# An expert layer in two chunks of 1792 features whose gate and up products share four PSUM banks, in place of four chunks with banks of their own

## The chip, the core and the metric

The kernel runs on one core of one Trainium2 chip. The metric is device time in microseconds (us) of one launch, the median of several runs. A change of under 0.2% (about 3 us here) can't be told from no change.

## The reference, cut to what matters

The reference is a trunk of two decoder layers over 256 tokens of width 1024. Each layer has a mixer (differential attention beside a gated DeltaNet) and a channel mixer: a dense SwiGLU in the first layer, and in the second a choice of two out of eight SwiGLU experts of 3584 features for each token. The change touches the experts alone.

```python
def swiglu(x, w_gate, w_up, w_down):
    return (jax.nn.silu(x @ w_gate) * (x @ w_up)) @ w_down

def moe_ffn(x, router_w, w_gate, w_up, w_down):
    ...
    logits = jnp.einsum('td,de->te', xf, router_w).astype(jnp.float32)
    top_val, top_idx = lax.top_k(logits, TOP_K)
    gates = jax.nn.softmax(top_val, axis=-1)
    ...
    def expert_block(args):
        tok_b, e_b = args
        xb = xf[tok_b]
        return swiglu(xb, w_gate[e_b], w_up[e_b], w_down[e_b])
    ...
    y = y * w_buf[:, None].astype(y.dtype)
    out = jax.ops.segment_sum(y, tok_buf, num_segments=T)
```

All weights are float32, and the eight experts hold 352 MB of them, each read once.

## The kernel before

**Numbers in two halves.** Products keep float32 accuracy by splitting both sides into a high and a low part of type float32r. A weight tile `raw` is loaded by a DMA on SyncE's queue (`load`), ScalarE copies it to the high part `wh` (L171), and VectorE subtracts to get the low part `wl` (L174). `halves` does this for one half of a load (2048 columns) at a time, so a half has 1024 columns, one ScalarE and one VectorE instruction, and `wpool` has four buffers for each part (`WB = 4`). For 128 tokens a half takes six matmuls of 512 columns: tokens high and low with `wh`, tokens high with `wl`.

**Jobs.** Each expert is a job. Five jobs are wide (128 slots for tokens). Three, the experts with the fewest tokens, are narrow: 64 slots, and high and low tokens lie side by side in one stationary tile of 128, so that a half takes four matmuls and not six. The sums of the two sides are joined later: ScalarE copies partitions 64 to 127 of a bank to SBUF (`lead`, L1099), and TensorE adds them to partitions 0 to 63 by a product with a shift matrix. The order of the jobs is wide, narrow, wide, narrow, wide, narrow, wide, wide (`TURN`).

**Chunks.** A job walks its 3584 features in chunks of 1024, 1024, 1024 and 512. For a chunk, all gate products run first into the banks `ps_mm`, then all up products into `ps_gd`. ScalarE takes SiLU of the gate banks into `hh` (L1144, L1148), VectorE multiplies `hh` with the up banks (L1155), TensorE transposes `hh` (L1168) into `ps_a`, and ScalarE and VectorE split the result into `hT` (L1170, L1171). The down products of a chunk (`down`, banks `ps_b`) are run one chunk later, mixed with the next chunk's transposes, so that TensorE has work while `hh` is made. In a narrow job the gate's leads run in the middle of the up products, when they are two or three pieces from their end.

**Dispatch and combine.** The tokens of a job are gathered by products with a 0/1 matrix `D` (`dispatch`, L99 `ps_a<-D,xs`, ScalarE copies to `xg`, L1016). It is called for a narrow and the following wide job at once, in eight steps that follow each other without other work between them, after the third chunk of the job before. `combine` scatters a finished job's sum back into `x_tok`.

**What sets the order.** The code is written in the order above. A scheduler may interleave instructions that don't depend on each other; an instruction marked with `pin` keeps its place on its engine. Each engine works its own list in order, so an instruction that waits holds up all behind it. Loads go through 13 buffers of 8 KB for each partition (`RING` and `RING2`).

Of the kernel before, what the change touches and what calls it, by code (L numbers as in the profile page):

```python
# [16 lines left out]
P = 128  # L17
# [20 lines left out]
RING2 = 6  # L38
SLOTS = "rrrrrxxxrrxxx"
CHUNKS = (1024, 1024, 1024, 512)  # L40
# [25 lines left out]
def trunk(ctx, tc, x, positions, w_in, conv_w, a_log, dt_bias, gdn_norm_w, lam_q1, lam_k1, lam_q2, lam_k2,  # L66
# [742 lines left out]
    def gate_pieces():  # L809

        n = 2048 // CHUNKS[0]
        wg = moe_w_gate[0, 0].rearrange("(k p) c -> p k c", p=P)
        return [piece(wg[:, k:k + n, 0:CHUNKS[0]], n, CHUNKS[0]) for k in (0, n)]

# [49 lines left out]
    def route(pl, mp):  # L864
# [8 lines left out]
        tie = mp.tile([P, NE, NE], F32, tag="hT0", name="tie")  # L873
# [101 lines left out]
    def experts(xs, jobs, mp, ring2, rest, first):  # L975
# [3 lines left out]

        C2 = [(sum(CHUNKS[:i]), n) for i, n in enumerate(CHUNKS)]  # L980

# [15 lines left out]
        def dispatch(group, early=False):  # L997
# [3 lines left out]
            Dt = mp.tile([P, NB, W], F32R, tag="hh", name=nm("D"))  # L1001
# [3 lines left out]
            for k in range(KD):  # L1005
# [11 lines left out]
            return xgs  # L1017

        def transposed(n):
            Dt = mp.tile([P, NB, P], F32R, tag="hh", name=nm("D"))  # L1020
# [8 lines left out]
        def in_pieces(w, c0, cols, parts=1, k0=0):  # L1029

            nk = 2048 // cols
            for k in range(k0, KD, nk):
                for j, wh, wl in piece(w[:, k:k + nk, c0:c0 + cols], nk, cols, parts):
                    yield k + j, nk // 2, wh, wl

        def products(outs, xg, narrow, k, nk, wh, wl, cols):

            if not narrow:
                xstat(outs, [xg[:, 0:4], xg[:, 4:8]], k, nk, 0, wh, wl, cols, KD)
                return  # L1040
            for j in range(nk):
                x_ = xg[:, k + j].rearrange("p c s -> p (c s)")
                for w in (wh, wl):
                    for i, o in enumerate(outs):
                        mm(o, x_, w[:, j * cols + i * 512:j * cols + (i + 1) * 512], k + j == 0 and w is wh, False)

        def down_pieces(e, c, parts=1, cut=1):
            wd = weights(e, 2).rearrange("(f p) d -> p f d", p=P)
            c0, cols = C2[c]
            for f in range(0, cols // P, 2):  # L1050
                last = f == cols // P - 2
                yield [(f + j, wh, wl) for j, wh, wl in piece(wd[:, c0 // P + f:c0 // P + f + 2, :], 2, D, parts,
                                                              cut if last else 1)]

        def down(subs, n, c, hT, py):
            f0 = C2[c][0] // P
            for f, wh, wl in subs:
                if jobs[n][3]:
                    x_ = hT[:, f].rearrange("p c s -> p (c s)")
                    for w in (wh, wl):  # L1060
                        for i, o in enumerate(py):
                            mm(o, x_, w[:, i * 512:(i + 1) * 512], f0 + f == 0 and w is wh,
                               f0 + f == FE // P - 1 and w is wl)
                else:
                    for w in (wh, wl):
                        for c_ in range(2 if w is wh else 1):
                            for i, o in enumerate(py):
                                mm(o, hT[:, f, c_], w[:, i * 512:(i + 1) * 512], f0 + f == 0 and w is wh and c_ == 0,
                                   f0 + f == FE // P - 1 and w is wl)

        def combine(n, q, py, DT):
            for i in range(2):
                ys = mp.tile([P, 2, 512], F32R, tag=f"hT{q % 2}", name=nm("ys"))
# [21 lines left out]
        def lead(p, room, i):  # L1095
# [8 lines left out]
        q = 0  # L1104
        xgs = dict(zip(groups[0], dispatch([jobs[n] for n in groups[0]], True)))
        groups.pop(0)
# [302 lines left out]
```

## Time and profile before

| what | value |
|---|---|
| median of 3 runs | 1533.79 us (1531.84 to 1534.95) |
| the profiled execution's own time | 1530.45 us |
| its span, first to last instruction | 1528.3 us |
| mean granted TensorE clock | 0.979 of full speed |

The span is the time between the first and the last instruction that the profiler saw; about 2 us lie around it. Engines are PE (TensorE; PEld is its weight load), DVE (VectorE), ACT (ScalarE) and SP (SyncE, which issues the loads). The expert layer takes the span from about 533 us to 1508 us.

### The profile page before, as it was taken

The page shows a single profiled execution, that of the slowest core. Times are in us where ns is not written, and L with a number is a line of the kernel's source. Part 1 is how long each engine was busy: PE and PEld are TensorE (multiplying, and loading weights), DVE is VectorE, ACT ScalarE, POOL GpSimd, SP SyncE. Part 2 cuts the span into 40 slices and gives each one's busy share as a digit, 9 for nine tenths or more (in the row PEclk, how much of TensorE's full clock was granted, in tenths as well). Part 3 has the DMA queues.
Part 4 walks back from the last instruction along what each step waited for, and adds up shares of the span by engine and source line. Part 5 has one row for each costly group of instructions (what it writes and reads, how often), then busy time and mean ns, then how long its engine had stood idle before and what let it go on. Part 6 is the DMA issues. An engine that isn't in the chain of part 4 may idle for free.

```text
span 1528.3 us, 23267 instructions
## 1 busy us (share of the span) xinstructions
PE 1459.9 (96%) x8522; PEld 1164.7 (76%) x8522; DVE 1248.0 (82%) x1553; ACT 1079.5 (71%) x1494; POOL 23.7 (2%) x36
## 2 busy tenths in 40 slices
PE   7989999999999999999999999999999999999996
PEld 7968899998978888765577775677776567877774
DVE  5787754556797889799999799999879999888996
ACT  3747544456657477788887788887778987777773
POOL 1000000000000000000000000000000000000000
PEclk8999999999999899999999999999999999999998
DMA  9623465545533589799999999999989999998960
GB/s 310 213 90 111 148 212 192 188 124 188 192 112 139 221 296 399 293 372 364 407 389 347 350 354 357 402 409 345 347 322 350 403 408 350 381 331 325 346 239 32
DMA packets 135522, 433.89 MB, mean 284 GB/s; under 512 B 7368, under 2 KB 9544, under 8 KB 135392
## 3 DMA queue, kind: packets, MB, share of 16 engines
q1 hardware_dynamic: 134208, 428.54, 75.7%
q0 software_dynamic: 1184, 3.71, 0.9%
q8 instruction: 71, 1.16, 0.3%
q14 instruction: 59, 0.48, 0.1%
HBM read 431.17 MB, written 1.05 MB: 283 GB/s over the span
## 4 chain that ended last, share of the span: by engine, by line
PE 82%; DVE 9%; ACT 4%; issue 2%; DMA 2%; SPq 0%; DVEq 0%; ACTq 0%
PE ps_gd L99 25%; PE ps_mm L99 25%; PE ps_b L99 21%; PE ps_a L99 9%; DVE wl L174 5%; ACT wh L171 2%; DMA raw<-in_moe_w_up_dram 1%; PE ps_a L1168 1%; DMA x_in<-in_x_dram 1%; DVE hT L1171 1%; DVE hh L1155 1%; DVE x_in L1082 1%; ACT xg L1016 0%; PE ps_mm L560 0%; DVE ys L1076 0%
## 5 line engine op out<-in xcount | busy, mean ns | idle before, releaser
L174 DVE TENSOR_TENSOR wl<-raw,wh 128x1024 fp32r<-128x1024 f32 (+1 forms) x811 | 956.7, 1218 | 154.0 <-ACT wh L171 148.9
L171 ACT ACTIVATE wh<-raw 128x1024 fp32r<-128x1024 f32 (+1 forms) x811 | 830.6, 1055 | 242.2 <-PE ps_gd L99 94.8
L99 PE MATMUL ps_b<-wh,hT 128*128 128x512 f32 x816 | 235.1, 400 | 0.3
L99 PE MATMUL ps_mm<-wh,xg 128*128 128x512 f32 x728 | 216.3, 404 | 2.4 <-ACT wh L171 2.4
L99 PE MATMUL ps_gd<-wh,xg 128*128 128x512 f32 x728 | 207.3, 394 | 0.0
L99 PEld LDWEIGHTS ps_b<-wh,hT 128*128 128x128 f32 x816 | 151.6, 189 | 38.1 <-ACT wh L171 3.1
L99 PE MATMUL ps_b<-wl,hT 128*128 128x512 f32 x492 | 164.3, 414 | 10.0 <-DVE wl L174 9.7
L99 PEld LDWEIGHTS ps_mm<-wh,xg 128*128 128x128 f32 x728 | 138.8, 193 | 35.1 <-ACT wh L171 4.1
L99 PEld LDWEIGHTS ps_gd<-wh,xg 128*128 128x128 f32 x728 | 136.7, 188 | 31.7
L99 PE MATMUL ps_mm<-wl,xg 128*128 128x512 f32 x448 | 150.1, 412 | 9.6 <-DVE wl L174 9.5
L99 PE MATMUL ps_gd<-wl,xg 128*128 128x512 f32 x448 | 148.3, 408 | 0.8 <-DVE wl L174 0.7
L99 PEld LDWEIGHTS ps_b<-wl,hT 128*128 128x128 f32 x492 | 86.7, 190 | 47.8 <-DVE wl L174 32.5
L99 PEld LDWEIGHTS ps_mm<-wl,xg 128*128 128x128 f32 x448 | 82.6, 192 | 47.4 <-DVE wl L174 31.2
L99 PEld LDWEIGHTS ps_gd<-wl,xg 128*128 128x128 f32 x448 | 80.3, 188 | 38.0 <-DVE wl L174 18.2
L99 PE MATMUL ps_mm<-xT,wh 128*128 128x256 f32 x448 | 70.9, 280 | 0.0
L1170 ACT ACTIVATE hT<-ps_a 128x512 fp32r<-128x512 f32 (+1 forms) x47 | 27.3, 583 | 53.5 <-PE ps_a L1168 53.3
L99 PEld LDWEIGHTS ps_mm<-xT,wh 128*128 128x128 f32 x448 | 60.8, 189 | 0.4
L1155 DVE TENSOR_TENSOR hh<-hh,ps_gd 128x512 f32<-128x512 f32 (+1 forms) x56 | 36.2, 681 | 26.3 <-PE ps_gd L99 21.8
L99 PE MATMUL ps_gd<-xT,wh 128*128 128x256 f32 x320 | 50.5, 280 | 0.0
L99 PE MATMUL ps_mm<-xT,wl 128*128 128x256 f32 x224 | 44.7, 280 | 0.0
L99 PEld LDWEIGHTS ps_gd<-xT,wh 128*128 128x128 f32 x320 | 43.1, 189 | 0.0
L1171 DVE TENSOR_TENSOR hT<-ps_a,hT 128x512 fp32r<-128x512 f32 (+1 forms) x47 | 31.2, 667 | 14.3 <-ACT hT L1170 14.3
(400 smaller groups left out, 1562.7 us busy)
## 6 DMA issues: line engine op xcount, KB each, us to landing
raw<-in_moe_w_gate_dram SPq DMA_DIRECT2D x110, 1024.0 KB, 6.5
raw<-in_moe_w_up_dram SPq DMA_DIRECT2D x110, 1024.0 KB, 7.6
raw<-in_moe_w_down_dram SPq DMA_DIRECT2D x110, 1024.0 KB, 8.2
raw<-in_w_in_dram SPq DMA_DIRECT2D x24, 1024.0 KB, 6.0
raw<-in_ffn_w_gate_dram SPq DMA_DIRECT2D x11, 1024.0 KB, 5.1
raw<-in_ffn_w_up_dram SPq DMA_DIRECT2D x11, 1024.0 KB, 5.2
raw<-in_ffn_w_down_dram SPq DMA_DIRECT2D x11, 1024.0 KB, 4.9
raw<-in_w_out_dram SPq DMA_DIRECT2D x8, 1024.0 KB, 4.8
```

What stands on the lines that cost most here:

```text
L99: return PE.matmul(o, lhsT, rhs, start=start, stop=stop, skip_group_check=True)
L171: high = S.activation(wh[:, c:c + n], w, AF.Copy)
L174: low = V.tensor_tensor(wl[:, c:c + n], w, wh[:, c:c + n].bitcast(F32), op=ALU.subtract)
L1082: V.scalar_tensor_tensor(o, pt, jobs[n][2][:, b], o, op0=ALU.mult, op1=ALU.add)
L1155: pin(V.tensor_tensor(h, h, p[rows, :], op=ALU.mult))
L1168: PE.transpose(pt[:, f * w:(f + 1) * w], hh[rows, (f0 + f) * P:(f0 + f + 1) * P], ident[rows, rows])
L1170: S.activation(hT[:, f0:f0 + n_, 0], pv, AF.Copy)
L1171: V.tensor_tensor(hT[:, f0:f0 + n_, 1], pv, hT[:, f0:f0 + n_, 0].bitcast(F32), op=ALU.subtract)
```

## The change

The features of a job are walked in two chunks of 1792. A gate or up load is one row block of 128 by 1792 (7 KB in one run for each partition), cut into two halves of 896, and a matmul has 448 columns. Gate and up use the same four banks (`ps_mm` twice and `ps_gd` twice), one after the other: the up products of a chunk can begin when SiLU has read the gate's banks. Three pieces of the former chunk's down products stand between gate and up, four after up. The leads of a narrow job move from the middle of the up products to the end of the gate and the end of the up (`leads`, two buffers `room`). A down load takes two neighbouring rows for each partition (8 KB in one run), which needs features in another order: the transposes read every 14th column of `hh`. The eight steps of a dispatch are put one by one behind the pieces of the job's last up products, and the transposes behind the pieces of the next gate products (`side`). `hT` is no longer double, and the load buffers are 12 instead of 13.

```diff
-RING2 = 6
-SLOTS = "rrrrrxxxrrxxx"
-CHUNKS = (1024, 1024, 1024, 512)
+RING2 = 5
+SLOTS = "rrrrrxxxrrxx"
+CHUNK = 1792
+BANK = CHUNK // 4
...
+        def in_pieces(w, c, k0=0):
+
+            for k in range(k0, KD):
+                yield k, piece(w[:, k:k + 1, c * CHUNK:(c + 1) * CHUNK], 1, CHUNK)
...
+            wd = weights(n, 2)[c * CHUNK:(c + 1) * CHUNK].rearrange("(p j) d -> p j d", j=NF)
...
+        def leads(banks):
 
             hi = slice(64, P)
-            o = room[hi, i * 512:(i + 1) * 512]
-            pin(S.activation(o, p[hi, :], AF.Copy))
-            return lambda: mm(p[0:64, :], shift[hi, 0:64], o, False, True)
+            moves = []
+            for p in banks:
+                o = mp.tile([P, BANK], F32R, tag="room", name=nm("room"), bufs=2)
+                pin(S.activation(o[hi], p[hi, :], AF.Copy))
+                moves.append(lambda o=o, p=p: mm(p[0:64, :], shift[hi, 0:64], o[hi], False, True))
+            return moves
...
+            hv = hh[rows].rearrange("s (p j) -> s j p", j=NF)
...
+                    PE.transpose(pt[:, f * w:(f + 1) * w], hv[:, f0 + f], ident[rows, rows])
...
+        def gu_banks():
+            return [bank(t)[:, 0:BANK] for t in ("mm", "mm", "gd", "gd")]
...
+                moves = leads(banks) if narrow else ()
+                more()
+                for move in moves:
+                    move()
+                for i, p in enumerate(banks):
+                    pin(S.activation(hh[rows, i * BANK:(i + 1) * BANK], p[rows, :], AF.Silu))
+                more()
+                more()
+                banks = gu_banks()
+                if c == NC - 1 and groups and n + 1 not in xgs:
+                    group = groups.pop(0)
+                    tiles, side = dispatch([jobs[g] for g in group])
+                    xgs.update(zip(group, tiles))
+                for sub in in_pieces(wu, c):
+                    products(banks, xg, narrow, *sub)
+                    if side:
+                        side.pop(0)()
...
+                moves = leads(banks) if narrow else ()
+                more()
+                for move in moves:
+                    move()
+                for i, p in enumerate(banks):
+                    h = hh[rows, i * BANK:(i + 1) * BANK]
+                    pin(V.tensor_tensor(h, h, p[rows, :], op=ALU.mult))
                 for subs in downs:
                     down(subs, *pend)
```

Place one is ScalarE's list in the first narrow job, its second chunk; `wh` rows are conversions, copies to `hT` (before) or `room` (changed) are leads, rows to `hh` are SiLU. Before, this is the stretch around the end of the up products:

```order
L1099 ACTIVATE hT_1005_7066<-ps_mm_1000_7061 64x512
L1099 ACTIVATE hT_1005_7066<-ps_mm_1001_7062 64x512
L171 ACTIVATE wh_1042_7197<-raw_1041_7195 128x1024
L171 ACTIVATE wh_1044_7207<-raw_1041_7195 128x1024
L171 ACTIVATE wh_1047_7217<-raw_1046_7215 128x1024
L171 ACTIVATE wh_1049_7221<-raw_1046_7215 128x1024
L1144 ACTIVATE hh_1004_7065<-ps_mm_1000_7061 64x512
L1144 ACTIVATE hh_1004_7065<-ps_mm_1001_7062 64x512
L1099 ACTIVATE hT_1005_7066<-ps_gd_1002_7063 64x512
L1099 ACTIVATE hT_1005_7066<-ps_gd_1003_7064 64x512
L171 ACTIVATE wh_1052_7243<-raw_1051_7241 128x1024
L171 ACTIVATE wh_1054_7247<-raw_1051_7241 128x1024
```

In the changed kernel this is the stretch around the end of the gate products (`raw_1124` and later are down pieces):

```order
L173 ACTIVATE wh_1125_7495<-raw_1124_7493 128x1024
L1101 ACTIVATE room_1120_7485<-ps_mm_1073_7316 64x448
L1101 ACTIVATE room_1121_7487<-ps_mm_1074_7317 64x448
L173 ACTIVATE wh_1127_7499<-raw_1124_7493 128x1024
L1101 ACTIVATE room_1122_7489<-ps_gd_1075_7318 64x448
L1101 ACTIVATE room_1123_7491<-ps_gd_1076_7319 64x448
L1165 ACTIVATE hh_1119_7484<-ps_mm_1073_7316 64x448
L1165 ACTIVATE hh_1119_7484<-ps_mm_1074_7317 64x448
L1165 ACTIVATE hh_1119_7484<-ps_gd_1075_7318 64x448
L1165 ACTIVATE hh_1119_7484<-ps_gd_1076_7319 64x448
L173 ACTIVATE wh_1130_7521<-raw_1129_7519 128x1024
L173 ACTIVATE wh_1132_7525<-raw_1129_7519 128x1024
```

The gate's two leads stood four conversions ahead of the SiLU that needs them. Now all four leads and all four SiLU stand together, with a single conversion among them, and the third lead can begin only when the first has been read by TensorE, since there are two `room` buffers.

Place two is VectorE's list in the same chunk, around the product of `hh` with the up banks. Before:

```order
L174 TENSOR_TENSOR wl_1048_7218<-raw_1046_7215,wh_1047_7217 128x1024
L174 TENSOR_TENSOR wl_1050_7222<-raw_1046_7215,wh_1049_7221 128x1024
L1155 TENSOR_TENSOR hh_1004_7065<-hh_1004_7065,ps_gd_1002_7063 64x512
L1155 TENSOR_TENSOR hh_1004_7065<-hh_1004_7065,ps_gd_1003_7064 64x512
L174 TENSOR_TENSOR wl_1053_7244<-raw_1051_7241,wh_1052_7243 128x1024
```

Changed (`wl_1182` is the last up half; `wl_1189` and `wl_1191` are down halves, whose `wh` stands behind two leads on ScalarE's list):

```order
L176 TENSOR_TENSOR wl_1182_7696<-raw_1178_7685,wh_1181_7695 128x896
L176 TENSOR_TENSOR wl_1189_7714<-raw_1187_7711,wh_1188_7713 128x1024
L176 TENSOR_TENSOR wl_1191_7718<-raw_1187_7711,wh_1190_7717 128x1024
L1185 TENSOR_TENSOR hh_1119_7484<-hh_1119_7484,ps_mm_1139_7555 64x448
L1185 TENSOR_TENSOR hh_1119_7484<-hh_1119_7484,ps_mm_1140_7556 64x448
L1185 TENSOR_TENSOR hh_1119_7484<-hh_1119_7484,ps_gd_1141_7557 64x448
L1185 TENSOR_TENSOR hh_1119_7484<-hh_1119_7484,ps_gd_1142_7558 64x448
L176 TENSOR_TENSOR wl_1194_7740<-raw_1192_7737,wh_1193_7739 128x1024
```

The product stands behind two down halves in both, and has four instructions and not two.

Place three is TensorE's list in a dispatch for a narrow and a wide job. Before, all 32 matmuls stand in one row; the first eight of them:

```order
L99 MATMUL ps_a_882_6565<-D_879_6560,xs0_5508 128x192
L99 MATMUL ps_a_882_6565<-D_879_6560,xs1_5509 128x192
L99 MATMUL ps_a_882_6565<-D_879_6560,xs0_5508 128x192
L99 MATMUL ps_a_882_6565<-D_879_6560,xs1_5509 128x192
L99 MATMUL ps_a_883_6572<-D_879_6560,xs0_5508 128x192
L99 MATMUL ps_a_883_6572<-D_879_6560,xs1_5509 128x192
L99 MATMUL ps_a_883_6572<-D_879_6560,xs0_5508 128x192
L99 MATMUL ps_a_883_6572<-D_879_6560,xs1_5509 128x192
```

Changed, in the next such dispatch, the first of its steps between two up pieces:

```order
L101 MATMUL ps_gd_1412_8628<-wh_1420_8647,xg_855_6439 128x448
L101 MATMUL ps_gd_1413_8629<-wh_1420_8647,xg_855_6439 128x448
L101 MATMUL ps_gd_1412_8628<-wl_1421_8648,xg_855_6439 128x448
L101 MATMUL ps_gd_1413_8629<-wl_1421_8648,xg_855_6439 128x448
L101 MATMUL ps_a_1422_8657<-D_1414_8630,xs0_5508 128x192
L101 MATMUL ps_a_1422_8657<-D_1414_8630,xs1_5509 128x192
L101 MATMUL ps_a_1422_8657<-D_1414_8630,xs0_5508 128x192
L101 MATMUL ps_a_1422_8657<-D_1414_8630,xs1_5509 128x192
L101 MATMUL ps_mm_1410_8626<-wh_1424_8666,xg_855_6439 128x448
L101 MATMUL ps_mm_1411_8627<-wh_1424_8666,xg_855_6439 128x448
L101 MATMUL ps_mm_1410_8626<-wh_1424_8666,xg_855_6439 128x448
L101 MATMUL ps_mm_1411_8627<-wh_1424_8666,xg_855_6439 128x448
```

Four matmuls of the dispatch now follow twelve of the up products, eight times.

## Rows read from the trace of the kernel before

**Rows 1.** The page, part 1: busy time, share of the span and instructions of each engine.

```profile
PE 1459.9 (96%) x8522; PEld 1164.7 (76%) x8522; DVE 1248.0 (82%) x1553; ACT 1079.5 (71%) x1494; POOL 23.7 (2%) x36
```

**Rows 2.** Busy time of each engine (count) in nine stretches, from one SiLU to the next.

```profile
core 0: us, PE busy (x) PEld busy (x) DVE busy (x) ACT busy (x) POOL busy (x), PEclk, DMA share, GB/s
612.88:644.04 31.16, 29.37 (x138) 24.00 (x137) 22.00 (x22) 21.99 (x37) 0.00 (x0) 0.95 0.74 271
819.53:854.00 34.47, 34.47 (x156) 28.00 (x155) 31.30 (x30) 26.53 (x30) 0.00 (x0) 1.00 1.00 377
854.00:883.86 29.86, 28.00 (x138) 22.44 (x137) 22.00 (x22) 21.88 (x37) 0.00 (x0) 1.00 0.83 304
912.84:943.01 30.17, 27.32 (x109) 17.62 (x108) 28.29 (x30) 24.99 (x29) 0.00 (x0) 1.00 0.92 344
943.01:974.00 30.99, 29.91 (x112) 18.64 (x111) 29.79 (x30) 28.02 (x31) 0.00 (x0) 0.94 1.03 401
974.00:996.83 22.83, 21.74 (x81) 13.88 (x80) 21.14 (x21) 19.01 (x22) 0.00 (x0) 0.93 1.03 409
996.83:1027.95 31.12, 30.46 (x127) 22.50 (x126) 29.47 (x27) 25.93 (x27) 0.00 (x0) 1.00 1.03 409
1094.17:1125.63 31.46, 29.61 (x138) 23.85 (x136) 22.00 (x22) 21.98 (x37) 0.00 (x0) 0.95 0.78 289
1335.55:1363.80 28.25, 27.73 (x137) 22.29 (x136) 21.79 (x21) 20.55 (x30) 0.00 (x0) 1.00 0.87 321
```

**Rows 3.** Chain that ended last, in order of time, one wide chunk: start, us, what.

```profile
833.97 11.12 PE ps_mm L99 x48
```

**Rows 4.** TensorE in order of time, dense stage, 256-column matmuls: start, us.

```profile
301.06 0.64 PE L99 MATMUL ps_gd<-xT,wh 128*128 128x256 f32 x4
301.54 0.40 PE L99 MATMUL ps_gd<-xT,wl 128*128 128x256 f32 x2
301.78 0.64 PE L99 MATMUL ps_gd<-xT,wh 128*128 128x256 f32 x4
```

**Rows 5.** Groups by line and form, 540 to 1500 us, VectorE.

```profile
L174 DVE TENSOR_TENSOR wl<-raw,wh 128x1024 fp32r<-128x1024 f32 x662 | 776.0, 1217 | 49.0 <-ACT wh L171 47.9
...
L1155 DVE TENSOR_TENSOR hh<-hh,ps_gd 64x512 f32<-64x512 f32 x21 | 13.5, 676 | 14.5 <-PE ps_gd L99 14.5
```

**Rows 6.** The same for ScalarE.

```profile
L171 ACT ACTIVATE wh<-raw 128x1024 fp32r<-128x1024 f32 x663 | 676.4, 1056 | 112.8 <-PE ps_mm L99 45.1 <-PE ps_gd L99 33.4 <-DVE wl L174 15.0
...
L1099 ACT ACTIVATE hT<-ps_gd 64x512 fp32r<-64x512 f32 x21 | 11.5, 590 | 1.6 <-PE ps_gd L99 1.1
```

**Rows 7.** Groups by line, whole span.

```profile
L1168 PEld LDWEIGHTS ps_a<-cst,hh 128*128 128x128 f32 (+1 forms) x224 | 24.0, 140 | 10.1 <-DVE hh L1155 4.2 <-issue 1.1
...
L799 DVE TENSOR_TENSOR hT<-sg,hT 128x256 fp32r<-128x256 f32 x20 | 8.4, 420 | 0.8 <-ACT hT L798 0.6
```

**Rows 8.** All engines in order of time, end of a narrow job's second up phase.

```profile
935.50 10.31 DVE L174 TENSOR_TENSOR wl<-raw,wh 128x1024 fp32r<-128x1024 f32 x9
...
943.88 0.62 PE L99 MATMUL ps_gd<-wl,xg 128*128 128x512 f32 x2
...
944.37 1.08 ACT L1099 ACTIVATE hT<-ps_gd 64x512 fp32r<-64x512 f32 x2 [0.29 <-PE ps_gd L99]
...
945.48 2.01 ACT L171 ACTIVATE wh<-raw 128x1024 fp32r<-128x1024 f32 x2
...
946.53 0.67 PE L99 MATMUL ps_gd<-hT,shift 64*64 64x512 f32 x2
947.01 1.28 DVE L1155 TENSOR_TENSOR hh<-hh,ps_gd 64x512 f32<-64x512 f32 x2 [1.20 <-PE ps_gd L99]
```

**Rows 9.** All engines in order of time, inside a dispatch.

```profile
871.08 0.52 PEld L99 LDWEIGHTS ps_a<-D,xs 128*128 128x128 f32 x4 [0.87 <-ACT xg L1016]
...
872.47 0.97 PEld L99 LDWEIGHTS ps_a<-D,xs 128*128 128x128 f32 x8 [0.87 <-ACT xg L1016]
```

**Rows 10.** Who waited for whom, 560 to 1500 us: total, times, longest.

```profile
ACT wh L171 <- DMA raw<-in_moe_w_up_dram: 0.6, 2, 0.3
```

More of the change, by code (lines that the diff above doesn't have):

```diff
@@ L1004, in dispatch, with part @@
             xgs = [xg_tile(job[3]) for job in group]
-            for k in range(KD):
+            def part(k):
                 pt = bank("ab"[k % 2] if early else "a")
@@ new lines, in products @@
+        def products(outs, xg, narrow, k, parts):
+            for i, (_, wh, wl) in enumerate(parts):
+                o = outs[2 * i:2 * i + 2]
+                if not narrow:
+                    xstat(o, [xg[:, 0:4], xg[:, 4:8]], k, 1, 0, wh, wl, CHUNK // 2, KD)
+                    continue
+                x_ = xg[:, k].rearrange("p c s -> p (c s)")
+                for w in (wh, wl):
+                    for j in range(2):
+                        mm(o[j], x_, w[:, j * BANK:(j + 1) * BANK], k == 0 and w is wh, False)
@@ L1055, in down, with down_pieces @@
+        def down_pieces(n, c, first=0, parts=1, cut=1):
+            wd = weights(n, 2)[c * CHUNK:(c + 1) * CHUNK].rearrange("(p j) d -> p j d", j=NF)
+            for f in range(first, NF, 2):
+                yield [(f + j, wh, wl) for j, wh, wl in piece(wd[:, f:f + 2, :], 2, D, parts, cut if f == NF - 2 else 1)]
         def down(subs, n, c, hT, py):
-            f0 = C2[c][0] // P
             for f, wh, wl in subs:
+                K, k = NC * NF, c * NF + f
                 if jobs[n][3]:
@@ new lines, in experts, with more @@
+            for c in range(NC):
+                banks = gu_banks()
+                for k, f in enumerate(first or ()):
+                    products(banks, xg, narrow, k, f)
+                for sub in in_pieces(wg, c, len(first or ())):
+                    products(banks, xg, narrow, *sub)
+                    if side:
+                        side.pop(0)()
+                first = None
+                fence[0] = fence_high[0] = None
+                while side:
+                    side.pop(0)()
+                hh = mp.tile([P, CHUNK], F32, tag="hh", name=nm("hh"))
+                downs = down_pieces(pend[0], pend[1]) if pend else iter(())
+                def more():
@@ new lines, in experts @@
+                for sub in in_pieces(wu, c):
+                    products(banks, xg, narrow, *sub)
+                    if side:
+                        side.pop(0)()
+                while side:
+                    side.pop(0)()
+                moves = leads(banks) if narrow else ()
[5 more added lines that the diff above has]
+                    pin(V.tensor_tensor(h, h, p[rows, :], op=ALU.mult))
@@ L1175, in experts @@
                 for subs in downs:
                     down(subs, *pend)
[L1177 to L1179 removed]
+                if pend and pend[1] == NC - 1:
+                    combine(pend[0], pend[3], DT)
+                if c == 0:
                     DT = transposed(n)
[L1181 removed]
                     py = [bank("b"), bank("b")]
[L1183 to L1185 removed]
+                hT, side = to_features(hh, narrow)
@@ L1186, in experts @@
                 pend = (n, c, hT, py)
-                q += 1
         _, where, gate, _ = job
-        f0 = C2[c][0] // P
-        subs = [(f0 + f, wh, wl) for subs in down_pieces(n, c, 2, 2) for f, wh, wl in subs]
+        while side:
+            side.pop(0)()
+        f0 = c * NF
+        TAIL = 4
+        for subs in itertools.islice(down_pieces(n, c), (NF - TAIL) // 2):
+            down(subs, *pend)
+        subs = [(f0 + f, wh, wl) for subs in down_pieces(n, c, NF - TAIL, 2, 2) for f, wh, wl in subs]
```

140 lines of the change are left out of this document (36 added, 104 removed).

## The prediction

> **What bounds the kernel now.** I read the page's part 1 first: TensorE is busy for 96% of the span, VectorE for 82%, ScalarE for 71% [rows 1]. That is an average over stages with different limits, so I cut the expert layer into stretches from one SiLU to the next and read the busy times [rows 2]. Three kinds show. In a wide job's chunk (819.53 to 854.00) TensorE is busy for 34.47 us of 34.47; the chain that ended last runs through unbroken rows of matmuls there, 48 in 11.12 us, or 0.2317 us each [rows 3]. 144 of these and eight transposes of 0.140 [rows 7] make 34.48: nothing waits. A narrow job's chunk (the four stretches from 912.84 to 1027.95) belongs to VectorE, idle for only 1.88, 1.20, 1.69 and 1.65 us, 6.42 in all; TensorE loses little more there because VectorE feeds it. The DMA share is high too (0.92 to 1.03, 344 to 409 GB/s), yet ScalarE, which takes the loads first, waits for an up load 0.6 us in all, in two waits [rows 10]. The third kind is the stretch with a dispatch: TensorE is busy for 29.37 of 31.16 us, VectorE for only 22.00.
>
> So the change is priced in wide jobs by what TensorE does, in narrow ones by what VectorE does or waits for.
>
> **The change part by part.** The sum is made against the profiled execution's own time, 1530.45 us; the median, 1533.79, lies 3.3 above it.
>
> *1. Dispatch between pieces.* Inside a dispatch TensorE stops for 0.87 us before four or eight weight loads of 0.121 us (0.97 for eight), because ScalarE's copy to `xg` must free the bank [rows 9]. Such a stretch needs 96 x 0.2317 + 8 x 0.140 + 32 x 0.121 = 27.2 us of TensorE. The four last 31.16, 29.86, 31.46 and 28.25 [rows 2], an excess of 3.9, 2.6, 4.2 and 1.0: 11.7 us. With twelve up matmuls (2.4 us) between two steps, the 0.87 us copy is covered, and I take all of it: **-11.7**. At worst half stays: -6.
>
> *2. 448 columns for 512 in wide jobs.* Gate and up of a job go from 336 matmuls of 512 to 384 of 448. A 256-column matmul in the dense stage takes 0.120 us (starts 301.06, 301.54, 301.78: six in 0.72) [rows 4]. On a line through 0.120 and 0.2317, 448 columns cost 0.2038: 78.26 us against 77.85, +0.41 in each of five jobs: **+2.0**. A little more fixed cost would make it 4.5; purely by columns it is 0.
>
> *3. 896 columns for 1024 on VectorE.* Back to back, nine subtractions of 1024 take 10.31 us, 1.146 each [rows 8]; one of 256 columns takes 0.420 [rows 7]. (The mean over all is 1.217 [rows 5]; I use the back-to-back value, and by the mean the term grows to about 4.) The slope gives 1.013 for 896. A narrow job's 64 gate and up halves then cost 64.8 us, where 56 cost 64.2: +0.65 in three jobs: **+2.0**. Purely by columns it is 0, so the term lies between 0 and 4. ScalarE's 1.056 [rows 6] changes in the same way, but has room.
>
> *4. Transitions in narrow jobs: the largest term.* Before, at the end of an up phase (936 to 956 us, [rows 8]) the last up matmul starts at 943.88 us, two leads follow on ScalarE (1.08 us from 944.37), two shift matmuls at 946.53, and VectorE's product at 947.01. VectorE had two down halves to do meanwhile and idles for 1.20. The gate's leads and SiLU cost it nothing: they ran while up products went to other banks. Afterwards gate and up share banks, so each chunk has two transitions on the path, four in a job where there were four already, but each with four leads and four SiLU or products, and with the conversions for VectorE queued behind them.
>
>  - Gate to up: ScalarE's list (place one) is one conversion, two leads, one conversion, two leads, four SiLU, then the next conversion. A lead of 448 columns takes about 0.53 (0.590 for 512 [rows 6]), a SiLU, whose rows I don't show, I take as long. The third lead needs the first's `room`, so a shift matmul must come between. VectorE gets two halves (2.0 to 2.3 us of work) out of ScalarE in a stretch that costs ScalarE 2 x 1.056 + 8 x 0.53 + one or two hand-overs to TensorE of some 0.4 (what is left of the 0.87 in [rows 9] once a copy of about half a microsecond is taken off), close to 7. Of the excess, what VectorE had in stock (four `wh` buffers) covers about half. By hand: about 3.2 us idle in the second chunk, 2.2 in the first, where wide downs (six matmuls a half) stand between.
>  - Up to gate: VectorE's list (place two) has two down halves ahead of the four products. Their `wh` stand behind two leads each on ScalarE, and the third lead again behind a shift. I work out 1.7 + 0.75 = 2.45 us idle, twice.
>
>  That is 10.3 us of idle per job for 6.42: +3.9 in three jobs: **+11.7**. At best ScalarE's stock hides the added part, and it is 0 here; at worst nothing covers a transition, 12.4 per job, +18.
>
> *5. Transitions in wide jobs.* SiLU of the first two banks can start before the last gate half ends on the other two; the other two SiLU and the next conversion, 2 x 0.53 + 1.056, end about 2.1 us after the gate's end, and the down piece ahead of it covers 12 x 0.2317 = 2.8. The cover is complete: **0**. If a conversion more stands in between, the 2.8 is overrun by some 0.35, and with a hand-over of 0.4 that is up to 0.7 at each of ten transitions: +7.
>
> *6. Job 0's first chunk* has no former chunk, hence no downs between gate and up: TensorE waits for four SiLU and a first conversion. I count **+1** above what it loses now (0 to 5).
>
> *7. The end.* The last chunk's 14 transposes and their splits have no next gate to lie behind; before, the last chunk had four. Ten more transposes with their copies, 1.4 us of loads and some hand-over: **+2** (0 to 4).
>
> *8. Transposes at a stride.* `hh` is now the stationary side read every 14th column, 56 bytes apart. The contiguous load takes 0.140 us [rows 7]; no strided one stands in this trace. Of 224, 140 lie in wide jobs, on TensorE's path. The ends are 0 (the load takes no notice of the stride) and a doubling, 140 x 0.140 = 19.6. The nearest row is the contiguous load itself, and loads can lie beside the matmul ahead (PEld is busy for 76% of the span [rows 1]), so I choose a value near the lower end, 25 ns each: **+3.5**.
>
> [...]
>
> *9. Loads* of 7 and 8 KB runs, in 12 buffers for 13: ScalarE waits on loads for 0.6 us in all [rows 10], so longer runs can win next to nothing: **0**. The lost buffer shortens a stock that is hardly ever empty.
>
> Nothing else is on a path: `hT` in one copy is free before its next write, since all seven down pieces precede it.
>
> Sum: -11.7 + 2.0 + 2.0 + 11.7 + 0 + 1 + 2 + 3.5 = +10.5, so 1530.45 becomes 1541, and beside the median 1544.3. I give **1543**, a little below, because terms 4 and 7 are worked out without what the scheduler may slip in.
>
> **The rivals.**
>
> *A, the forecast* (1538 to 1552): VectorE's idle time in a narrow job rises to about 10.
>
> *B, the strided load costs its full price.* Term 8 is then 19.6 instead of 3.5: 1543 + 16 = 1559. For it: TensorE has no slack in a wide chunk [rows 2], so what a transpose takes more is paid in full. Against it: the 140 ns load can lie beside the matmul ahead of it. [...]
>
> *C, faster: the shared banks cost VectorE nothing.* ScalarE has room in narrow chunks (24.99 busy of 30.17, 28.02 of 30.99 [rows 2]). If the conversions ahead of a transition keep VectorE in stock, as they do now at 943.88, then only the up-to-gate transition stays, 1.6 us each as now (6.42 / 4), two a job: 3.2 us for 6.42. Term 4 turns from +11.7 to -9.6, and the time is 1543 - 21.3 = 1522. It decides at 5.8 us of idle per narrow job (term 4 below -2, with which and a dispatch gain of 11.7 the sum is below -3); above 7.8 the kernel is slower.
>
> *D, balance* (1531 to 1537): idle around 6.5 to 7.5 per narrow job, or the dispatch pays and the rest is half of what I work out.
>
> **How the numbers follow.** A .46, B .09, C .27, D .18. What can be told from no change is 0.2%, 3 us. A and B are slower, C faster, D the same: .55, .27, .18. The range runs from 1518 (C with term 8 at its lower end, 0) to B's 1559; what lies outside is a fifth or less, of C where the small terms vanish too and of B with term 4 at its worst. The forecast's own range is 1538 to 1552.
>
> **What would show it.** Steps 1 and 9: no stops of 0.87 us before dispatch weight loads, and ScalarE's waits on loads still around 1 us. Step 2: 48 matmuls of 448 columns in about 9.8 us. Step 4: VectorE's idle time in the three narrow jobs near 10 us each, ended by `wh`, by the third lead and by the bank of up products; near 3 would show C. Step 5: no idle of TensorE ended by SiLU in wide jobs. Step 8: the strided `LDWEIGHTS` beside 140 ns, and the spacing of transposes in wide jobs. The forecast is wrong if ScalarE's stock of `wh` outlasts a transition, if the dispatch hides little, or if a strided load takes double.

## The result

The changed kernel takes 1540.52 us (median of 8 runs, 1536.79 to 1546.4) against 1532.82 for the kernel before; the ratio is 1.0062 [1.0047, 1.0076], some 9.5 us (7.2 to 11.6) more (the two medians lie 7.7 apart). The prediction said slower, 1543. Its sum is near in part by luck: the dispatch gave back more than forecast and the narrow jobs lost more, and these two errors have opposite signs.

The profiled execution of the changed kernel is the longest of the eight (own time 1546.4, granted clock 0.973; the others 0.976 to 0.981). Its page, part 1, beside [rows 1]: TensorE, VectorE and ScalarE are a little busier in microseconds and no busier in share; the weight loads (PEld) go from 76% to 80%.

```profile
PE 1471.1 (95%) x8864; PEld 1239.8 (80%) x8864; DVE 1253.9 (81%) x1630; ACT 1092.3 (71%) x1577; POOL 23.6 (2%) x36
```

Busy time in stretches from SiLU to SiLU, as in [rows 2]: the two of a narrow job, then the two of the wide job behind it (the last holds a dispatch).

```profile
905.97:969.31 63.34, 58.10 (x244) 41.60 (x242) 57.27 (x61) 50.24 (x62) 0.00 (x0) 1.00 0.92 339
969.31:1028.51 59.20, 54.84 (x227) 43.23 (x227) 51.79 (x53) 47.28 (x56) 0.00 (x0) 0.91 0.96 371
1028.51:1088.35 59.84, 58.61 (x271) 48.37 (x270) 56.05 (x62) 48.37 (x57) 0.00 (x0) 1.00 0.95 359
1088.35:1151.93 63.58, 62.76 (x307) 52.83 (x305) 55.30 (x57) 52.50 (x74) 0.00 (x0) 1.00 0.97 368
```

VectorE idles 6.07 and 7.41 us in the first two, 13.48 against 6.42 before [rows 2]; TensorE idles 0.82 us in the whole stretch of 63.58 with the dispatch.

**The dispatch.** TensorE in order of time, one round of twelve up matmuls and a dispatch step:

```profile
852.17 0.97 PE L101 MATMUL ps_mm<-wh,xg 128*128 128x448 f32 x4
...
853.39 0.97 PE L101 MATMUL ps_gd<-wh,xg 128*128 128x448 f32 x4
...
854.60 0.59 PE L101 MATMUL ps_a<-D,xs 128*128 128x192 f32 x4
855.02 1.00 PE L101 MATMUL ps_mm<-wh,xg 128*128 128x448 f32 x4
```

Nothing stops. Four matmuls of a step take 0.42 us (854.60 to 855.02). Six matmuls of 448 columns take 1.22 (852.17 to 853.39), 0.203 each.

**The narrow job.** VectorE at the four transitions of the job: the end of the first gate, the first up, the second gate and the second up.

```profile
903.90 1.23 DVE L176 TENSOR_TENSOR wl<-raw,wh 128x1024 fp32r<-128x1024 f32 x1 [1.65 <-ACT wh L173]
905.98 1.22 DVE L176 TENSOR_TENSOR wl<-raw,wh 128x1024 fp32r<-128x1024 f32 x1 [0.85 <-ACT wh L173]
908.77 20.67 DVE L176 TENSOR_TENSOR wl<-raw,wh 128x1024 fp32r<-128x1024 f32 x20 [1.56 <-ACT wh L173]
931.29 1.23 DVE L176 TENSOR_TENSOR wl<-raw,wh 128x1024 fp32r<-128x1024 f32 x1 [1.86 <-ACT wh L173]
933.37 1.23 DVE L176 TENSOR_TENSOR wl<-raw,wh 128x1024 fp32r<-128x1024 f32 x1 [0.85 <-ACT wh L173]
...
968.33 1.22 DVE L176 TENSOR_TENSOR wl<-raw,wh 128x1024 fp32r<-128x1024 f32 x1 [0.52 <-ACT wh L173]
972.11 20.66 DVE L176 TENSOR_TENSOR wl<-raw,wh 128x1024 fp32r<-128x1024 f32 x20 [2.56 <-ACT wh L173]
994.64 1.23 DVE L176 TENSOR_TENSOR wl<-raw,wh 128x1024 fp32r<-128x1024 f32 x1 [1.87 <-ACT wh L173]
996.72 1.23 DVE L176 TENSOR_TENSOR wl<-raw,wh 128x1024 fp32r<-128x1024 f32 x1 [0.85 <-ACT wh L173]
```

4.06, 2.71, 3.08 and 2.72: 12.57 us of idle time, each ended by a conversion. (A row of several instructions names the form of the first; 2.5 of the 12.57 us lie ahead of the SiLU at 905.97, so 3.4 of the 13.48 lie elsewhere.) ScalarE at the first of them:

```profile
897.42 1.91 ACT L173 ACTIVATE wh<-raw 128x896 fp32r<-128x896 f32 x2 [0.27 <-DMA raw<-in_moe_w_up_dram]
901.82 0.97 ACT L1101 ACTIVATE room<-ps_mm 64x448 fp32r<-64x448 f32 x2 [2.49 <-PE ps_mm L101]
902.81 1.06 ACT L173 ACTIVATE wh<-raw 128x1024 fp32r<-128x1024 f32 x1
903.89 0.97 ACT L1101 ACTIVATE room<-ps_gd 64x448 fp32r<-64x448 f32 x2
```

ScalarE has nothing to do for 2.49 us: it stands at a lead that waits for the gate's last products, and the conversion for which VectorE starves stands right behind it. Over 560 to 1500 us, who waited for whom (total, times, longest), in the changed kernel and then, for the leads of the kernel before, there:

```profile
ACT room L1101 <- PE ps_mm L101: 26.2, 12, 2.7
```

```profile
ACT hT L1099 <- PE ps_mm L99: 4.3, 3, 1.4
ACT hT L1099 <- PE ps_gd L99: 1.1, 4, 0.3
```

Twelve waits, one at each transition of three narrow jobs, and 26.2 us where 5.4 stood.

### The profile page after: what moved, and what is told of

Same layout as the page of the kernel before. It is cut to its first block, busy times and chain, and to the rows that moved or that the text cites. A ratio compares the mean times of both kernels' runs of the same rounds, so it can differ in the third digit from the quotient of the medians.

```text
span 1544.4 us, 24332 instructions
## 1 busy us (share of the span) xinstructions
PE 1471.1 (95%) x8864; PEld 1239.8 (80%) x8864; DVE 1253.9 (81%) x1630; ACT 1092.3 (71%) x1577; POOL 23.6 (2%) x36
## 3 DMA queue, kind: packets, MB, share of 16 engines
HBM read 431.17 MB, written 1.05 MB: 280 GB/s over the span
## 5 line engine op out<-in xcount | busy, mean ns | idle before, releaser
L176 DVE TENSOR_TENSOR wl<-raw,wh 128x896 fp32r<-128x896 f32 (+2 forms) x875 | 962.1, 1142 | 192.5 <-ACT wh L173 175.0
L173 ACT ACTIVATE wh<-raw 128x896 fp32r<-128x896 f32 (+2 forms) x875 | 844.9, 995 | 242.2 <-PE ps_gd L101 89.5
L101 PE MATMUL ps_gd<-wh,xg 128*128 128x448 f32 x832 | 223.7, 367 | 0.0
L101 PE MATMUL ps_mm<-wh,xg 128*128 128x448 f32 x832 | 218.8, 371 | 1.0 <-ACT hh L1165 1.0
L101 PEld LDWEIGHTS ps_gd<-wh,xg 128*128 128x128 f32 x832 | 156.4, 188 | 13.9
L101 PE MATMUL ps_gd<-wl,xg 128*128 128x448 f32 x512 | 153.5, 380 | 4.8 <-DVE wl L176 1.2
L101 PE MATMUL ps_mm<-wl,xg 128*128 128x448 f32 x512 | 151.1, 373 | 3.3 <-DVE wl L176 3.0
L1119 ACT ACTIVATE hT<-ps_a 128x512 fp32r<-128x512 f32 (+2 forms) x52 | 27.5, 540 | 22.1 <-PE ps_a L1117 15.2
L1117 PEld LDWEIGHTS ps_a<-cst,hh 128*128 128x128 f32 (+1 forms) x224 | 32.2, 201 | 6.9 <-DVE hh L1185 4.1
L1120 DVE TENSOR_TENSOR hT<-ps_a,hT 128x512 fp32r<-128x512 f32 (+2 forms) x52 | 31.8, 619 | 7.0 <-ACT hT L1119 6.9
```

The costliest lines, as they stand in the source:

```text
L101: return PE.matmul(o, lhsT, rhs, start=start, stop=stop, skip_group_check=True)
L173: high = S.activation(wh[:, c:c + n], w, AF.Copy)
L176: low = V.tensor_tensor(wl[:, c:c + n], w, wh[:, c:c + n].bitcast(F32), op=ALU.subtract)
L1117: PE.transpose(pt[:, f * w:(f + 1) * w], hv[:, f0 + f], ident[rows, rows])
L1119: S.activation(hT[:, f0:f0 + n_, 0], pv, AF.Copy)
L1120: V.tensor_tensor(hT[:, f0:f0 + n_, 1], pv, hT[:, f0:f0 + n_, 0].bitcast(F32), op=ALU.subtract)
```

## The experiments

Ratios are to the kernel before, timed beside each run, with 95% intervals; a difference between two runs in microseconds is the difference of their ratios times 1533. What is to be tested: spreading the dispatch gives time back, and leads at the end of both phases, with ScalarE's conversions behind them, take it again. Rivals are named with each.

**The dispatch, undone in the changed kernel.**

```diff
                 for sub in in_pieces(wu, c):
                     products(banks, xg, narrow, *sub)
-                    if side:
-                        side.pop(0)()
                 while side:
                     side.pop(0)()
```

> The changed kernel with one part undone: the eight steps of a dispatch follow each other without up pieces between them. Theory: in the trace of the changed kernel a round of twelve up matmuls and one dispatch step takes about 2.87 us and a round without a step 2.43, so four dispatches cost 4 x 8 x 0.44 = 14 us; in the kernel before they cost 27.3. Undoing it should give back the 13: ratio to the kernel before about 1.0062 + 0.0085 = 1.0147 (1.012 to 1.017), and stops before the dispatch's weight loads of 0.8 to 0.9 us in the trace. Rival: the stops were hidden by work left over from elsewhere, and spreading brought nothing; then 1.006 (1.004 to 1.008).

Measured: 1555.96 us, 1.0141 [1.0113, 1.0169], 12 us above the changed kernel. The scheduler still slipped six matmuls of the dispatch shown here in between earlier pieces; the other 26 stand together. TensorE there:

```profile
876.92 1.14 PE L101 MATMUL ps_a<-D,xs 128*128 128x192 f32 x8 [0.20 <-ACT xg L1019]
878.75 0.69 PE L101 MATMUL ps_a<-D,xs 128*128 128x192 f32 x4 [0.69 <-ACT xg L1019]
880.14 2.02 PE L101 MATMUL ps_a<-D,xs 128*128 128x192 f32 x8 [0.69 <-ACT xg L1019]
```

The stops are back, two of them 0.69 us long. Busy times of the stretch that follows show one thing more: the clock granted from 880 to 887 us is 0.52.

```profile
880.00:887.00 7.00, 6.86 (x21) 5.76 (x22) 2.47 (x3) 3.17 (x9) 0.00 (x0) 0.52 0.74 279
```

**The dispatch alone, in the kernel before.** Its third chunk's up loop calls one step after each piece, and `hh` is taken after the loop, since `D` lies in its place.

```diff
                 for s, sub in enumerate(in_pieces(wu, c0, cols, parts)):
                     products(pu, xg, narrow, *sub, cols)
...
+                    if steps:
+                        steps.pop(0)()
```

> The kernel before with one part of the change alone: the eight steps of a dispatch stand one by one behind the pieces of the third chunk's up products. Theory: -13 us, ratio 0.9915 (0.989 to 0.994), and the stretches of 31.2, 29.9, 31.5 and 28.3 us between two SiLU fall to about 27. Rival (spreading brings nothing): 1.000 (0.998 to 1.002).

Measured: 1519.22 us, 0.9906 [0.988, 0.9931], 14 us less. The stretch of the third and fourth chunk's SiLU, 34.47 + 29.86 = 64.33 us in [rows 2], takes 61.09, with no idle TensorE:

```profile
817.48:878.57 61.09, 61.09 (x291) 50.37 (x290) 53.39 (x52) 48.10 (x65) 0.00 (x0) 1.00 0.99 361
```

Both runs agree with what was expected: this one part of the change is worth 12 to 14 us.

**Conversions ahead of the leads.** In narrow jobs the first down piece is issued first, at both transitions.

```diff
+                ahead = next(downs, None) if narrow else None
                 moves = leads(banks) if narrow else ()
-                more()
+                if ahead:
+                    down(ahead, *pend)
+                if not narrow:
+                    more()
```

> The changed kernel with another order in narrow jobs alone: at the end of a gate and of an up, the first down piece (its load and its two conversions on ScalarE) is issued ahead of the leads and not behind them. Theory: VectorE idles there because ScalarE stands at the leads, waiting 1.4 to 2.7 us for the last product, with the conversions queued behind; with two conversions ahead VectorE has 2.3 us of work meanwhile, and its idle time at the four transitions of a narrow job falls from 12.6 to some 6 us; three jobs give -15 to -20 us, ratio 0.994 (0.992 to 0.998). Rival: the four leads and four SiLU cost what they cost wherever they stand (their busy time on ScalarE, or the bank that TensorE waits for), and the idle time moves a few instructions later: 1.004 to 1.007.

Measured: 1526.73 us, 0.9955 [0.9938, 0.9973], 16 us below the changed kernel and faster than before. An order of issue alone turns the sign. In the traces VectorE's idle time in the three narrow jobs falls from 40.2 to 27.5 us, 12.7 of the 16; the rest was not traced. But the wait at the end of a gate hardly shrank:

```profile
898.68 2.36 DVE L176 TENSOR_TENSOR wl<-raw,wh 128x1024 fp32r<-128x1024 f32 x2 [3.56 <-ACT wh L173]
...
959.38 21.80 DVE L176 TENSOR_TENSOR wl<-raw,wh 128x1024 fp32r<-128x1024 f32 x21 [3.16 <-ACT wh L173]
```

3.56 and 3.16 us, for 4.06 and 3.08; VectorE's gain is in the two other transitions. What is left behind the gate could be the leads or the shared banks, which leaving out the leads tells apart.

**No leads**, in the changed kernel and in the kernel before: `moves = ()` for every call.

> The changed kernel without the leads and the shift products of narrow jobs (it leaves out the joining of the two token sides there, so 16 ScalarE copies and 16 TensorE products of a narrow job). Theory: the leads cost because ScalarE stands at them with the conversions behind; without them the conversions come first, and the time falls at least as far as with the conversions issued ahead (0.9955), to 0.990 to 0.995. Rival: most of what is lost in a narrow job is the wait of the shared banks for four SiLU, which stays; 1.000 to 1.004.

> The kernel before without the leads and shift products of narrow jobs (it leaves out the joining of the two token sides there). In the changed kernel leaving them out took 38 us off. Theory: the leads of the gate lie beside up products before, and those of the up delay VectorE's product by 1.2 to 1.9 us at four places of a narrow job; without them VectorE's idle time falls by 4 to 5 of 6.4 us in each: -12 to -15 us, ratio 0.991 (0.988 to 0.994); the rest of the 38, some 25, is what the change added in narrow jobs. Rival: the leads cost as much before (their work on TensorE and ScalarE, wherever it stands): 0.976 to 0.980.

Measured: the changed kernel without leads 1504.72 us, 0.981 [0.978, 0.9839], beyond what the theory had named; the kernel before without them 1520.31, 0.991 [0.9888, 0.9932], as expected. Leads and shift products thus cost 38.6 us after the change (1.0062 - 0.981) and 13.8 before: the change added 24.8, uncertain by about 6 (the intervals). VectorE without leads in the changed kernel, at the ends of the two gates:

```profile
890.18 22.95 DVE L176 TENSOR_TENSOR wl<-raw,wh 128x1024 fp32r<-128x1024 f32 x22 [0.23 <-ACT wh L173]
...
947.76 22.94 DVE L176 TENSOR_TENSOR wl<-raw,wh 128x1024 fp32r<-128x1024 f32 x22 [0.24 <-ACT wh L173]
```

0.23 and 0.24 us, and no wait before VectorE's products behind the two up phases. Its idle time in this narrow job is 2.9 us where it was 13.48; in the kernel before it falls from 6.42 to 2.0. The shared banks and four SiLU cost VectorE next to nothing; the rival falls. These two runs also leave out the work of the leads, so they price leads and waits together; the order of issue alone gave back 16. Without leads on either side the changed kernel is 0.010 faster, some 15 us and uncertain by 6: the dispatch's 12 to 14 cover it, and all else that was changed comes to nothing that shows.

**Four buffers for the leads**, the third and fourth copy in the tile of `combine`.

```diff
-            for p in banks:
-                o = mp.tile([P, BANK], F32R, tag="room", name=nm("room"), bufs=2)
+            more_room = mp.tile([P, 2, 512], F32R, tag="ys", name=nm("room"))
+            for i, p in enumerate(banks):
+                if i < 2:
+                    o = mp.tile([P, BANK], F32R, tag="room", name=nm("room"), bufs=2)
+                else:
+                    o = more_room[:, i - 2, 0:BANK]
```

> The changed kernel with four buffers for the leads' copies and not two (the third and fourth in the tile that combine and dispatch use). The prediction counted hand-overs at the third lead, which needs the first's buffer. Theory: in the trace of the changed kernel the third lead starts right after the conversion that stands between the pairs, later than the first shift product, so the buffers make nobody wait: 1.006 (1.004 to 1.008). Rival: the hand-over counts at the transitions, 0.4 us at twelve: 1.003.

Measured: 1541.03 us, 1.0051 [1.0034, 1.0069]. Not told from the changed kernel: the buffers hold up nobody there.

**Features in their old order.**

```diff
-            wd = weights(n, 2)[c * CHUNK:(c + 1) * CHUNK].rearrange("(p j) d -> p j d", j=NF)
+            wd = weights(n, 2)[c * CHUNK:(c + 1) * CHUNK].rearrange("(j p) d -> p j d", p=P)
...
-                    PE.transpose(pt[:, f * w:(f + 1) * w], hv[:, f0 + f], ident[rows, rows])
+                    PE.transpose(pt[:, f * w:(f + 1) * w], hh[rows, (f0 + f) * P:(f0 + f + 1) * P], ident[rows, rows])
```

> The changed kernel with features in their old order: the transposes read 128 neighbouring columns of hh, and a down load takes two rows 128 apart (two runs of 4 KB). Theory: nothing to be had; the strided load is recorded at 0.197 to 0.207 us against 0.140, but four transposes follow in 0.38 us in both, so 35 groups could lose 1 us at most; ratio 1.006 (1.004 to 1.008). Rival (the stride costs its full price on TensorE's path, 140 x 0.140 us): 16 to 20 us less, 0.994. A second rival, that runs of 8 KB are worth something to the loads: a slower kernel, 1.008 or more.

**The stride kept, runs of 4 KB.** A down load takes rows j and j + 7 of a partition.

```diff
-            wd = weights(n, 2)[c * CHUNK:(c + 1) * CHUNK].rearrange("(p j) d -> p j d", j=NF)
-            for f in range(first, NF, 2):
-                yield [(f + j, wh, wl) for j, wh, wl in piece(wd[:, f:f + 2, :], 2, D, parts, cut if f == NF - 2 else 1)]
+            H = NF // 2
+            wd = weights(n, 2)[c * CHUNK:(c + 1) * CHUNK].rearrange("(p a j) d -> p j a d", a=2, j=H)
+            for f in range(first // 2, H):
+                yield [(f + H * j, wh, wl) for j, wh, wl in piece(wd[:, f], 2, D, parts, cut if f == H - 1 else 1)]
```

> The changed kernel with one part of the other feature order alone: the transposes keep reading every 14th column, and a down load takes two rows of a partition that are seven apart, in two runs of 4 KB in place of one of 8. With features in their old order the time was 0.0044 lower (ratio 1.0018). Theory: that came from the transposes (a strided transpose needs the products of all four banks, a contiguous one those of one bank), and runs of 4 KB cost nothing: 1.006 (1.004 to 1.008). Rival: the shorter runs were what helped: 1.002 (1.000 to 1.0035).

Measured: the old order 1536.6 us, 1.0018 [1.0, 1.0037]; the runs of 4 KB 1542.45, 1.0053 [1.0036, 1.007]. The first missed: I expected no difference from the changed kernel, and it is 6.7 us below it, though not by the 16 to 20 of the rival. The second puts this down to the transposes and not to the loads. Where it lies, the second up's end in the changed kernel shows:

```profile
998.57 0.63 PE L101 MATMUL ps_b<-wh,hT 128*128 128x512 f32 x2
1000.12 1.88 PE L1117 MATMUL ps_a<-cst,hh 64*128 64x64 f32 x14 [0.92 <-DVE hh L1185]
...
1003.80 1.05 PE L101 MATMUL ps_b<-wl,hT 128*128 128x512 f32 x2
1004.65 1.05 PE L101 MATMUL ps_b<-wh,hT 128*128 128x512 f32 x2
...
1009.73 0.96 PE L101 MATMUL ps_mm<-wh,xg 128*128 128x448 f32 x4
```

and the same place with the old order:

```profile
994.39 0.63 PE L101 MATMUL ps_b<-wh,hT 128*128 128x512 f32 x2
994.95 1.45 PE L1116 MATMUL ps_a<-cst,hh 64*128 64x64 f32 x14
...
1003.31 0.99 PE L101 MATMUL ps_mm<-wh,xg 128*128 128x448 f32 x4
```

A transpose of every 14th column reads all four products of VectorE, so the first of them waits 0.92 us for the last; a transpose of 128 neighbours reads those of one or two, and the first starts at once. Then TensorE's clock falls. The stretch behind it, in the changed kernel and then in the old order:

```profile
1000.90:1007.70 6.80, 6.80 (x24) 5.43 (x23) 6.80 (x7) 3.32 (x4) 0.00 (x0) 0.51 0.90 341
```

```profile
994.90:1001.70 6.80, 5.99 (x32) 3.82 (x31) 6.80 (x8) 5.42 (x6) 0.00 (x0) 1.00 0.91 330
```

Two matmuls of 512 columns take 0.85 us (1003.80 to 1004.65) and not 0.46. From the last down products ahead of the transposes to the first of the wide job's gate it is 11.16 us (998.57 to 1009.73) in the changed kernel and 8.92 (994.39 to 1003.31) in the old order: 2.2 lost. At the two other narrow jobs' ends it is 1.5 and 2.6. The clock is not a matter of the stop alone: in the changed kernel it is 0.50 or 0.51 over 6.8 us behind all three, but in the old order, too, it is 0.51 over 3.4 us behind the first, where the transposes start at once. From first SiLU to first SiLU the three narrow jobs take 365.84 us in the changed kernel and 358.55 in the old order, 7.3 less; the three wide jobs that follow them take 369.93 and 369.83. All of the difference is in the narrow jobs.

**What is left behind the gate.** Three more, each on the one before: the old order beside conversions ahead; then the second down piece, too, issued ahead of the shift products and SiLU; then four buffers for the leads.

> Both edits that gained in narrow jobs: the first down piece issued ahead of the leads, and features in their old order. Theory: the old order gained mostly by letting TensorE go on at the end of a narrow job, where its clock then fell for 3.4 us and not for 6.8; with the conversions ahead that stretch is 3.4 us already, so little is left: 0.9945 (0.992 to 0.996). Rival: the strided load itself costs, in all jobs alike; then both add up, 0.991.

> The same, and between gate and up of a narrow job the second down piece's conversions too are issued ahead of the shift products and SiLU. Theory: 3.2 to 3.6 us of VectorE's idle time at each of these six transitions are left, since four SiLU stand ahead of the next conversion; with two conversions more VectorE has 2.3 us more to do: down to 1 to 1.5 us each, -10 us, ratio 0.988 (0.985 to 0.991). Rival: what is left is TensorE's wait for the shared banks, and a later SiLU only makes it longer: 0.994 or above.

> The kernel with two down pieces ahead and the old feature order (0.9931), and four buffers for the leads. Theory: there the third lead does wait, 1.3 us, for the first shift product, which stands behind a down piece on TensorE; with buffers enough the leads follow each other, VectorE's 3.56 us at the end of a first gate fall by 1 to 2, and up to gate likewise by less: -4 to -8 us, 0.9895 (0.987 to 0.992). Rival: the shift products themselves and SiLU set the next conversion: 0.993.

Measured: 1525.35 us, 0.9942 [0.9919, 0.9965]; 1524.12, 0.9931 [0.9907, 0.9955]; 1518.55, 0.9892 [0.9871, 0.9913]. The first is as expected: not told from conversions ahead alone (0.9955). The second missed: the 3.56 us stayed. In its trace, ScalarE at the end of the first gate:

```profile
896.01 2.01 ACT L173 ACTIVATE wh<-raw 128x1024 fp32r<-128x1024 f32 x2
899.36 0.97 ACT L1101 ACTIVATE room<-ps_gd 64x448 fp32r<-64x448 f32 x2 [1.34 <-PE ps_mm L101]
```

The third lead waits 1.34 us for a buffer, which the first shift product frees, and that one stands behind a down piece on TensorE. So a cause that makes nobody wait in the changed kernel appears once the first is mended. The third run is as expected, 0.0039 below the second (uncertain by 0.0032). With four buffers VectorE's waits there become

```profile
897.35 2.36 DVE L176 TENSOR_TENSOR wl<-raw,wh 128x1024 fp32r<-128x1024 f32 x2 [0.38 <-ACT wh L173]
901.39 20.67 DVE L176 TENSOR_TENSOR wl<-raw,wh 128x1024 fp32r<-128x1024 f32 x20 [1.68 <-ACT wh L173]
```

**A second piece ahead in the kernel before with spread dispatch.**

```diff
+                    second = next(downs, None)
                     moves = [lead(p, room, i) for i, p in enumerate(pu)]
...
-                    subs = next(downs, None)
-                    if subs:
-                        down(subs, *pend)
+                    if second:
+                        down(second, *pend)
```

> The kernel before with dispatch steps between up pieces (ratio 0.9906), and in narrow jobs the second down piece too issued ahead of the up's leads. Theory: VectorE idles 1.2 to 1.9 us there after two down halves; with four it has 2.3 us more, and three jobs give up to -12 us: 0.985 (0.982 to 0.988). Rival: no more than four wh and wl buffers exist, so the conversions can't run further ahead: 0.9906 (0.989 to 0.993).

Measured: 1520.4 us, 0.991 [0.9888, 0.9933]: nothing beyond 0.9906. The rival's outcome, but the trace shows another course than the rival's:

```profile
DVE hh L1169 <- PE ps_gd L99: 11.8, 20, 1.0
DVE hT L1184 <- ACT hT L1183: 14.8, 16, 1.6
```

VectorE's waits for the up products do fall, from 21.3 us with the spread dispatch alone to 11.8, but those for ScalarE's copies to `hT`, which come next, rise from 7.9 to 14.8. Most of the idle time has moved; the number of `wh` buffers was not tried.

Of the versions that leave nothing out, the two fastest are the changed kernel with its narrow jobs mended (0.9892) and the kernel before with the dispatch spread (0.9906). Their intervals overlap.

## Why the prediction was right, and where it was not

- *Dispatch* (-11.7): right, perhaps a little small; -12 undone, -14 alone. What a dispatch lost before were stops (0.87 us in [rows 9]), and in two of four stretches a clock below 1 as well (0.95 in [rows 2]).
- *448 columns* (+2.0): 0.2025 to 0.203 us each (twelve in 2.43, six in 1.22), as worked out (0.2038) or a little less; 384 of them are 77.8 to 78.1 against 77.85. So the term is 0 to +1.
- *896 columns on VectorE* (+2.0): near. Over 540 to 1500 us, beside the first line of [rows 5]:

```profile
L176 DVE TENSOR_TENSOR wl<-raw,wh 128x896 fp32r<-128x896 f32 x508 | 528.7, 1087 | 32.9 <-ACT wh L173 20.9 <-PE ps_mm L101 0.6
```

 By busy time 64 halves of 1.041 us (528.7 / 508) take 66.6, where 56 of 1.172 took 65.6: +1.0 a job, +3 in three. (The prediction's 1.013 takes its slope from the duration 1.217; through the two values it names, 1.146 and 0.420, the line gives 1.025, and the term would be +4.)
- *Transitions in narrow jobs* (+11.7): right in kind, somewhat small, and not by the path that was worked out. Three of the four were near: 2.71, 2.72 and 3.08 for 2.45, 2.45 and 3.2. The weakest step is the end of the first gate, "2.2 in the first": 4.06. There I let the stock of `wh` cover half, and took wide downs for cover; but ScalarE stands still for 2.49 us at the first lead, VectorE uses up the stock meanwhile, and the conversions of those downs are what stands behind the lead. That the other three are near is in part luck: the term counted ScalarE's work and hand-overs at the third lead, and had no wait at the first lead, 26.2 us in twelve; the hand-overs hold up nobody there, as four buffers showed, and four SiLU and the shared banks cost next to nothing once the leads are gone. The sum also set 10.3 us at transitions against all idle time before, 6.42. All idle time after is 13.48, +7.1 a job and 21 in three, of which the strided transposes take 6 to 7 (below). That leaves 14 to 15 for the leads, where the runs without them give 24.8, uncertain by 6, with some of the transposes' cost in it.
- *Wide transitions* (0), *job 0* (+1): right. TensorE runs on through a wide transition; in the whole span one SiLU of the experts keeps it waiting, in job 0's first chunk, for 1.05 us:

```profile
559.42 0.68 PE L101 MATMUL ps_mm<-wh,xg 128*128 128x448 f32 x2 [1.05 <-ACT hh L1165]
```

- *The end* (+2): one stop of 0.69 us at 1502.93 waits for `hT`; the rest of the term was not measured apart.
- *Strided transposes* (+3.5, and rival B): half of its size (5.4 to 6.7 us by the two runs on it, 7.3 by the traces), and the place wrong. By lines and forms, the wide jobs' loads, to be read beside [rows 7]:

```profile
L1117 PEld LDWEIGHTS ps_a<-cst,hh 128*128 128x128 f32 x140 | 21.8, 197 | 1.4 <-DVE hT L1120 0.4
```

 A load takes 197 ns for 140, but TensorE, idle for 0.82 us in the 63.58 of a wide job's second stretch, doesn't stop for it: the three wide jobs behind narrow ones take 0.1 us less in the old order. What shows is the loss at a narrow job's end, where a transpose waits for four products, 0.92 us at the second up's end. No run shows the doubling of rival B, which was the prediction's own assumption: the load takes 57 ns more and not 140, and TensorE hardly waits for it.
- *Loads* (0): right. Runs of 4 KB are not told from 8 KB.

The traces close the sum, though only of the two profiled executions. From the layer's first product to TensorE's last matmul they take 980.67 us before (532.98 to 1513.65) and 992.42 after (536.85 to 1529.27), 11.75 more; of the 16 us between the two, 3.9 lie ahead of the layer, where little more than the first two gate loads differs. Cut at the first SiLU of each job, the three narrow jobs go from 345.04 to 365.84, +20.8, with VectorE busy for 326.0 and 325.6: all of it is VectorE's idle time. The three wide jobs, each behind a narrow one, go from 379.7 to 369.9, -9.7, and the first and last job together take 0.7 more. (The cuts hold other shares of the neighbours' work before and after, so narrow and wide are parted roughly.) In the kernel before with spread dispatch the same wide jobs are 9.6 shorter and the first and last 4.5. So beside the dispatch the narrow jobs cost 20.8, for 13.7 forecast (terms 3 and 4), and the strided transposes' 7.3 are as large as the difference; these three wide jobs cost nothing, for some 3 (448 columns and strided transposes, 5.5 in five wide jobs); the first and last job cost 5, for 5 (terms 6 and 7, and two fifths of the 5.5). The errors of the narrow jobs, +7, and of the wide jobs and the dispatch, -3 and -2, partly cancel: that the sum came within 1 or 2 us is luck.

## What to carry to other kernels

An engine that stands at an instruction whose input is late idles with ready work behind it, as ScalarE did for 2.49 us at a lead; ask of every copy issued at a phase's end not what it takes but how long it waits at the head of its list, and issue there first what another engine will need meanwhile (16 us here). The dispatch's short steps, which hand a buffer back and forth between two engines, cost stops of 0.20 and 0.69 us in one row and, between long products, no stop beyond their own 0.42 us. Before a layout is made for longer loads, look at which writes each reader then depends on: runs of 8 KB were not told from 4 KB here, and the reader waited 0.92 us.

## What the runs showed of the hardware that was not expected

TensorE's granted clock falls to about half in two places behind stops and short instructions: the fourteen transposes at the end of a narrow job, behind a stop of 0.92 us (0.51 over 6.8 us), and the dispatch in one row, with stops of 0.69 (0.52 over 7 us). It then costs the long products that follow: two of 512 columns take 0.85 us and not 0.46. A stationary load of every 14th float32 column takes 197 ns against 140, and TensorE hardly waits for it (0.1 us in the three wide jobs).
